# Pairs of seven block products moved between pairs of eight, and their banks read during the last pair

## The chip, the cores and the metric

One core of a Trainium2 chip runs the whole program in one launch. The metric is the device time of one execution in microseconds (us); the time before is the median of three runs. Five engines work at their own pace: TensorE (matmuls and transposes; PE in the profile), VectorE (DVE), ScalarE (ACT), GpSimd (POOL) and SyncE (SP), which issues the loads. Each runs its instructions in the order in which the program has them, and waits where an operand or a buffer isn't ready.

## What is computed

Two layers, each a mixer (a gated recurrence, differential attention and latent attention, joined and projected) and a feed-forward block, on 256 rows of 2048 numbers. The change is in the feed-forward block alone:

```python
D_MODEL = 2048
SEQ = 256
DEPTH = 2
D_FF = -(-8 * D_MODEL // (3 * 256)) * 256      # 5632
...
for l in range(DEPTH):
    ...
    x = x + mix @ w_out[l]
    h = rmsnorm(x, g_ffn[l])
    x = x + (jax.nn.silu(h @ w_gate[l]) * (h @ w_up[l])) @ w_down[l]
return rmsnorm(x, g_final)
```

All of it is float32.

## The kernel before

**Products.** The 5632 hidden columns go in eleven blocks f0 to f10 of 512. For each block a *gate-up product* multiplies the 256 rows (two row tiles t = 0, 1 of 128) with 512 columns of `w_gate` and 512 of `w_up`, over 16 blocks of 128 inputs. Its result is turned around in `hidden()` by TensorE's transposes and stored as the left side of the *down products*. The hidden blocks are taken in groups 0 to 3, 4 to 7 and 8 to 10; after each group two down products (one for each half of the 2048 output columns, again as two halves of 512) add into `x`. Both kinds are written by `paired()`.

**Precision.** A number is split in a high part and a low rest (`whi`, `wlo`): ScalarE casts (L231), VectorE subtracts (L232), and `mm3()` makes three matmuls (L237 to L239). A matmul here has 128 rows of weights and 512 columns.

**Pairs.** A product takes its input blocks two at a time. A *pair of eight* makes the eight block products (two weights, two row tiles, two input blocks) with 24 matmuls, and needs two loads of 512 KB, each split by `load_split()`. A *pair of seven* makes seven block products with 21 matmuls: it takes weighted sums of the blocks of both sides. The sums of the left side are made once (`build_sums()`); those of the weights are made for each pair by VectorE (L345 to L348, half operations of 512 columns) and split (L349, L350, L352, L354), with ScalarE's casts between (L343, L344, L351, L353). A product with sevens has five pairs of eight and three of seven: 5 x 24 + 3 x 21 = 183 matmuls. f0 of each layer has eight pairs of eight (192 matmuls). The two down products after f10 have six pairs: the first all of eight (144), the second in layer 0 with two of seven (138); in layer 1 the last is another function. In all 86 pairs of seven, in 28 products of three and one of two. The loads and weight sums of such a product, 22 tiles, pass in turn through the six buffers of `wraw`; the parts of splits go through three buffers of `whl`; of the sums there are two sets for V and W (`A_SET`) and one for gate and up (`A_GU`).

**Banks.** TensorE adds up in banks of PSUM. `acc` has five: C11, C22, C21, C12 (one for each weight half and row tile) and P1; `aux` has three, P5, P7, P6, and serves the transposes as well. A product with sevens runs all its pairs of eight first and then its three sevens. C22 is complete after the eights, the others after the last seven; `ev()` reads them: for a gate-up product two copies and ten VectorE operations, which end in silu(gate) x up in `sil`, for a down product twelve additions.

**What sets the order.** TensorE's order is the program's own. The other engines' order is made by a scheduler when the kernel is built, which gives `tc.high_priority()` work precedence. Side work is done a step at a time: each `yield` of a product calls `tick()`, which runs one step of up to two generators of `side` (in the feed-forward block `hidden()`, whose second and third step transpose two blocks each, and `xT_steps()`, which prepares the next stage's left side).

Of the kernel before, what the change touches and what calls it, by code (L numbers as in the profile page):

```python
# [21 lines left out]
P = 128  # L22
D = 2048
T = 256
NT = 2
# [12 lines left out]
SEVEN_X, SEVEN_H = (5, 6, 7), (3, 4, 5)  # L38
ARENA1, ARENA2 = 14504, 2816
# [18 lines left out]
def body(ctx: ExitStack, tc: tile.TileContext, x_in, pos_in, pvec_in, lamv_in, cst_in, w_in, w_r, w_i, w_q_b,  # L58
# [109 lines left out]

    side = []
# [25 lines left out]
    def run(gen, ticks=None):  # L195
        for i, _ in enumerate(gen):
            if ticks is None or i < ticks:
                tick()
# [102 lines left out]
    def paired(wg, wu, order, seven, part, sums, ev):  # L301
# [7 lines left out]
        C11, C22, C21, C12 = (acc() for _ in range(4))  # L309
        bank = {(0, 0): C11, (1, 1): C22, (0, 1): C21, (1, 0): C12}  # L310
        plain = ((0, 0), (0, 1), (1, 0), (1, 1)) if not seven else ((0, 0), (1, 1), (0, 1), (1, 0))
# [5 lines left out]
        for i, p in enumerate(order):  # L317
            last = i == len(order) - 1
            hl = [load_split(w[2 * p * P:(2 * p + 2) * P], 2, (512,)) for w in (wg, wu)]
            for s, t in plain:  # L320
                hi, lo = hl[s]
                for j in range(2):
                    mm3(bank[s, t], part(2 * p + j, t), (hi[:, j], lo[:, j]), i == 0 and j == 0,
                        last and j == 1 and (not seven or (s, t) == (1, 1)))
                if last and not seven:
                    read((s, t), bank[s, t])
            if last and seven:
                read("C22", C22)
            yield
        if not seven:  # L330
            return
        P1 = acc()
        P5, P7, P6 = (aux() for _ in range(3))
        for i, p in enumerate(seven):
            e, o = 2 * p, 2 * p + 1
            G, U = (load(w[2 * p * P:(2 * p + 2) * P], 2, (512,)).rearrange("p (a b) -> p a b", a=2)
# [18 lines left out]
            first, end = i == 0, i == len(seven) - 1  # L355
            S1, S2, S3, S4 = sums(p)
            mm3(P1, part(e, 0), (gh[:, 0], gl[:, 0]), first, end)
            if end:
                read("P1", P1)
            mm3(C11, part(o, 0), (gh[:, 1], gl[:, 1]), False, end)  # L360
            if end:
                read("C11", C11)
            mm3(C12, S4, (uh, ul), False, end)
            mm3(P5, S1, (vh[:, 0], vl[:, 0]), first, end)
            mm3(P7, S3, (vh[:, 1], vl[:, 1]), first, end)
            mm3(P6, S2, (wh[:, 0], wl[:, 0]), first, end)
            if end:
                read("P6", P6, P7)
# [790 lines left out]
```

## Time and profile before

| | us |
|---|---|
| median of 3 runs | 2136.89 (2136.43 to 2139.54) |
| the profiled execution | 2142.38 |
| its span, first to last instruction | 2140.6 |
| layer 0, f1 to the last down product | 694.24 |
| layer 1, f1 to the last paired down product | 656.41 |

The profile lists each engine's busy time, who waited for whom, and the instructions in order of time. A matmul's end is modelled, and matmuls overlap; so two that start 0.23 us apart are both drawn 0.39 us long. A window row gives each engine's busy time in a stretch, with the number of its instructions in brackets. The products of layer 0 begin at 335.98 (f0), 381.42 (f1), 424.56 (f2), 469.50 (f3) and 514.38 us (first down product).

### The profile page before, as it was taken

How to read it: one execution, taken by the hardware profiler on the slowest of the kernel's cores; microseconds unless marked ns; L12 is line 12 of the kernel's file. 1: busy time of each engine (PE TensorE's matmuls, PEld its weight loads, DVE VectorE, ACT ScalarE, POOL GpSimd, SP SyncE). 2: the span in 40 equal slices, each digit the busy share in tenths (PEclk: the TensorE clock that was granted, in tenths of full speed). 3: DMA queues.
4: the chain of work that ended last, by engine and by line, in shares of the span. 5: the costliest groups of instructions: out<-in, count | busy, mean ns of one | idle time of the engine just before them, and what ended most of it. 6: DMA issues, size and time to landing. Idle time of an engine off the chain costs nothing.

```text
span 2140.6 us, 27189 instructions
## 1 busy us (share of the span) xinstructions
PE 2080.3 (97%) x10044; PEld 1727.0 (81%) x10044; DVE 1681.4 (79%) x2381; ACT 1174.0 (55%) x1622; POOL 14.9 (1%) x32
## 2 busy tenths in 40 slices
PE   8999999999999999999999999999999999999998
PEld 7898888877777777777798998887777777777786
DVE  5775756789898898988775756567889888999885
ACT  5764655556455564555647545455554555555554
POOL 0000000000000000000000000000000000000000
PEclk9999999999999999999999999999999999999999
DMA  7664456555556555565565645565555655556563
GB/s 243 172 181 134 159 175 187 190 186 174 187 187 210 190 170 189 185 206 188 171 192 159 193 126 169 180 181 194 169 183 187 206 195 174 184 185 217 190 213 132
DMA packets 204213, 391.17 MB, mean 183 GB/s; under 512 B 18960, under 2 KB 36384, under 8 KB 203952
## 3 DMA queue, kind: packets, MB, share of 16 engines
q1 hardware_dynamic: 204032, 389.36, 56.7%
q8 instruction: 78, 1.28, 0.2%
q14 instruction: 55, 0.45, 0.1%
q0 software_dynamic: 48, 0.09, 0.0%
HBM read 387.30 MB, written 2.10 MB: 182 GB/s over the span
## 4 chain that ended last, share of the span: by engine, by line
PE 52%; DVE 29%; DMA 11%; issue 5%; ACT 2%; DVEq 0%; SPq 0%; ACTq 0%; POOLq 0%; POOL 0%
PE acc L238 16%; PE acc L239 16%; PE acc L237 15%; DVE wlo L232 8%; DMA wraw<-in_w_up 6%; DMA wraw<-in_w_down 4%; DVE arena L352 2%; DVE arena L354 2%; DVE wraw L346 2%; ACT whi L231 2%; DVE wraw L347 2%; DVE wraw L345 2%; DVE arena L350 2%; DVE arena L349 2%; DVE wraw L348 1%
## 5 line engine op out<-in xcount | busy, mean ns | idle before, releaser
L232 DVE TENSOR_TENSOR wlo<-wraw,whi 128x1024 fp32r<-128x1024 f32 (+2 forms) x568 | 665.4, 1179 | 310.3 <-ACT whi L231 304.6
L231 ACT CAST whi<-wraw 128x1024 fp32r<-128x1024 f32 (+2 forms) x568 | 576.2, 1015 | 547.2 <-PE acc L239 389.6
L238 PE MATMUL acc<-wlo,xTh 128*128 128x512 f32 x1248 | 487.0, 390 | 24.0 <-DVE wlo L232 23.7
L237 PE MATMUL acc<-whi,xTh 128*128 128x512 f32 x1248 | 490.4, 393 | 0.0
L239 PE MATMUL acc<-whi,xTl 128*128 128x512 f32 x1248 | 482.8, 387 | 0.0
L238 PE MATMUL acc<-wlo,hTh 128*128 128x512 f32 (+1 forms) x784 | 307.6, 392 | 14.9 <-DVE wlo L232 14.9
L237 PE MATMUL acc<-whi,hTh 128*128 128x512 f32 (+1 forms) x784 | 309.3, 395 | 0.1
L239 PE MATMUL acc<-whi,hTl 128*128 128x512 f32 (+1 forms) x784 | 305.6, 390 | 0.0
L238 PEld LDWEIGHTS acc<-wlo,xTh 128*128 128x128 f32 x1248 | 234.8, 188 | 86.9 <-DVE wlo L232 42.9
L237 PEld LDWEIGHTS acc<-whi,xTh 128*128 128x128 f32 x1248 | 234.7, 188 | 45.3
L239 PEld LDWEIGHTS acc<-whi,xTl 128*128 128x128 f32 x1248 | 234.6, 188 | 45.4
L238 PEld LDWEIGHTS acc<-wlo,hTh 128*128 128x128 f32 x784 | 148.2, 189 | 50.9 <-DVE wlo L232 23.1
L237 PEld LDWEIGHTS acc<-whi,hTh 128*128 128x128 f32 x784 | 148.2, 189 | 30.7 <-issue 1.3
L239 PEld LDWEIGHTS acc<-whi,hTl 128*128 128x128 f32 x784 | 148.2, 189 | 29.4
L351 ACT CAST arena<-wraw 128x1024 fp32r<-128x1024 f32 x86 | 90.3, 1050 | 121.6 <-DVE wraw L346 121.5
L237 PE MATMUL acc<-xTh,whi 128*128 128x256 f32 x384 | 111.4, 290 | 1.9 <-ACT xTh L484 1.0
L349 DVE TENSOR_TENSOR arena<-wraw,arena 128x1024 fp32r<-128x1024 f32 x86 | 104.9, 1220 | 9.1 <-ACT arena L343 8.3
L343 ACT CAST arena<-wraw 128x1024 fp32r<-128x1024 f32 x86 | 90.3, 1050 | 37.7 <-PE acc L239 26.9
L238 PE MATMUL acc<-xTl,whi 128*128 128x256 f32 x384 | 109.0, 284 | 1.9 <-DVE xTl L485 1.9
L239 PE MATMUL acc<-xTh,wlo 128*128 128x256 f32 x384 | 108.8, 283 | 0.5 <-DVE wlo L232 0.5
L354 DVE TENSOR_TENSOR arena<-wraw,arena 128x1024 fp32r<-128x1024 f32 x86 | 105.2, 1223 | 0.0
L352 DVE TENSOR_TENSOR arena<-wraw,arena 128x1024 fp32r<-128x1024 f32 x86 | 104.8, 1219 | 0.0
(260 smaller groups left out, 2957.1 us busy)
## 6 DMA issues: line engine op xcount, KB each, us to landing
wraw<-in_w_gate SPq DMA_DIRECT2D x176, 512.0 KB, 4.3
wraw<-in_w_up SPq DMA_DIRECT2D x176, 512.0 KB, 4.6
wraw<-in_w_down SPq DMA_DIRECT2D x176, 512.0 KB, 4.6
wraw<-in_w_out SPq DMA_DIRECT2D x64, 512.0 KB, 3.8
wraw<-in_w_in SPq DMA_DIRECT2D x48, 512.0 KB, 4.2
wraw<-in_w_in SPq DMA_DIRECT2D x48, 384.0 KB, 3.2
wraw<-in_w_in SPq DMA_DIRECT2D x32, 416.0 KB, 3.5
arena<-in_w_in SPq DMA_DIRECT2D x16, 384.0 KB, 7.4
```

The lines of the kernel that those rows point to most:

```text
L231: nc.scalar.copy(hi[:, :n], raw[:, :n])
L232: nc.vector.tensor_tensor(lo[:, :n], raw[:, :n], hi[:, :n].bitcast(F32), ALU.subtract)
L237: nc.tensor.matmul(ps, a[0], b[0], start=start, stop=False)
L238: nc.tensor.matmul(ps, a[0], b[1], start=False, stop=False)
L239: nc.tensor.matmul(ps, a[1], b[0], start=False, stop=stop)
L343: nc.scalar.copy(fl(gh), fl(G))
L345: tt(V[:, 0], U[:, 0], G[:, 0], ALU.subtract)
L346: tt(V[:, 1], U[:, 1], U[:, 0], ALU.subtract)
L349: tt(fl(gl), fl(G), f_(fl(gh)), ALU.subtract)
L351: nc.scalar.copy(fl(vh), fl(V))
L352: tt(fl(vl), fl(V), f_(fl(vh)), ALU.subtract)
L354: tt(fl(wl), fl(W), f_(fl(wh)), ALU.subtract)
```

## The change

`SEQ` writes out the order of a product's pairs: with three sevens it is eight, eight, seven, eight, seven, eight, seven, eight (`OOSOSOSO`), and it ends with an eight. The four banks of a product are taken in the order in which they are used, (0, 0), (0, 1), (1, 0), (1, 1) (weight half, row tile), and every pair of eight fills them in that order; before, products with sevens went (0, 0), (1, 1), (0, 1), (1, 0). Within a seven the products of P6, P7 and P5 stand in that order. After the last seven P1, P6, P7 and P5 are joined (stage `"P"`), while TensorE does the last eight; each of the four banks is read when its part of that eight is done. The copy of C22 by ScalarE in gate-up products is gone; the numbers of VectorE operations are as before. Ticks: none after a seven and after an eight between sevens, one more in the middle of each product's second eight; so the two steps of `hidden()` with transposes come in the middle and at the end of the second eight.

```diff
 SEVEN_X, SEVEN_H = (5, 6, 7), (3, 4, 5)
+
+SEQ = {(8, 0): "OOOOOOOO", (6, 0): "OOOOOO", (6, 2): "OOSOSO", (8, 3): "OOSOSOSO", (8, 2): "OOSOOSOO"}
...
     def run(gen, ticks=None):
-        for i, _ in enumerate(gen):
-            if ticks is None or i < ticks:
+        for i, v in enumerate(gen):
+            if v is not False and (ticks is None or i < ticks):
                 tick()
...
-        C11, C22, C21, C12 = (acc() for _ in range(4))
-        bank = {(0, 0): C11, (1, 1): C22, (0, 1): C21, (1, 0): C12}
-        plain = ((0, 0), (0, 1), (1, 0), (1, 1)) if not seven else ((0, 0), (1, 1), (0, 1), (1, 0))
+        bank, ps = {}, []
 
         def read(stage, *banks):
             with tc.high_priority(offset=AHEAD):
                 ev(stage, *banks)
 
-        for i, p in enumerate(order):
-            last = i == len(order) - 1
+        def eight(i, p, last):
             hl = [load_split(w[2 * p * P:(2 * p + 2) * P], 2, (512,)) for w in (wg, wu)]
-            for s, t in plain:
-                hi, lo = hl[s]
-                for j in range(2):
-                    mm3(bank[s, t], part(2 * p + j, t), (hi[:, j], lo[:, j]), i == 0 and j == 0,
-                        last and j == 1 and (not seven or (s, t) == (1, 1)))
-                if last and not seven:
-                    read((s, t), bank[s, t])
-            if last and seven:
-                read("C22", C22)
-            yield
-        if not seven:
-            return
-        P1 = acc()
-        P5, P7, P6 = (aux() for _ in range(3))
-        for i, p in enumerate(seven):
+            for s in range(2):
+                for t in range(NT):
+                    if i == 0:
+                        bank[s, t] = acc()
+                    hi, lo = hl[s]
+                    for j in range(2):
+                        mm3(bank[s, t], part(2 * p + j, t), (hi[:, j], lo[:, j]), i == 0 and j == 0, last and j == 1)
+                    if last:
+                        read((s, t), bank[s, t])
+                if i == 1 and s == 0:
+                    yield
+
+        def seven_of(i, p, end):
             e, o = 2 * p, 2 * p + 1
+            if i == 0:
+                ps.extend([acc()] + [aux() for _ in range(3)])
+            P1, P6, P7, P5 = ps
...
             S1, S2, S3, S4 = sums(p)
-            mm3(P1, part(e, 0), (gh[:, 0], gl[:, 0]), first, end)
+            mm3(P1, part(e, 0), (gh[:, 0], gl[:, 0]), i == 0, end)
             if end:
                 read("P1", P1)
-            mm3(C11, part(o, 0), (gh[:, 1], gl[:, 1]), False, end)
+            mm3(bank[0, 0], part(o, 0), (gh[:, 1], gl[:, 1]), False, False)
+            mm3(bank[1, 0], S4, (uh, ul), False, False)
+            mm3(P6, S2, (wh[:, 0], wl[:, 0]), i == 0, end)
+            mm3(P7, S3, (vh[:, 1], vl[:, 1]), i == 0, end)
+            mm3(P5, S1, (vh[:, 0], vl[:, 0]), i == 0, end)
+            mm3(bank[0, 1], part(o, 1), (wh[:, 1], wl[:, 1]), False, False)
             if end:
-                read("C11", C11)
-            mm3(C12, S4, (uh, ul), False, end)
-            mm3(P5, S1, (vh[:, 0], vl[:, 0]), first, end)
-            mm3(P7, S3, (vh[:, 1], vl[:, 1]), first, end)
-            mm3(P6, S2, (wh[:, 0], wl[:, 0]), first, end)
-            if end:
-                read("P6", P6, P7)
-            mm3(C21, part(o, 1), (wh[:, 1], wl[:, 1]), False, end)
-            if end:
-                read("end", C21, C12, P5)
-            yield
+                read("P", P6, P7, P5)
+
+        todo = [*order]
+        done = 0
+        n = len(order) + len(seven)
+        for i in range(n):
+            if SEQ[n, len(seven)][i] == "S":
+                seven_of(done, seven[done], done == len(seven) - 1)
+                done += 1
+                yield False
+            else:
+                p = todo.pop(0)
+                for _ in eight(len(order) - len(todo) - 1, p, i == n - 1):
+                    yield
+                yield not 0 < done < len(seven)
...
+        q12, q22 = (at(A_U + i * 512, 512) for i in range(2))
 
         def ev(stage, a, b=None, c=None):
...
+            if stage == "P1":
+                nc.scalar.copy(sil[0], a)
+            elif stage == "P":
+                tt(q12, sil[0], a, ALU.add)
+                tt(sil[1], q12, b, ALU.add)
+                tt(q22, sil[1], c, ALU.add)
+                tt(q12, q12, c, ALU.add)
             else:
-                tt(sil[1], u3, a, ALU.add)
-                gate(1, sil[1])
-                tt(u2, u2, c, ALU.add)
-                tt(u2, u2, b, ALU.add)
-                tt(u3, u3, c, ALU.add)
-                tt(u3, u3, o22, ALU.add)
-                up(0, u2)
-                up(1, u3)
+                s, t = stage
+                if seven:
+                    v = (sil[t], q12 if t == 0 else q22)[s]
+                    tt(v, v, a, ALU.add)
+                    a = v
+                if s == 0:
+                    nc.scalar.activation(sil[t], a, AF.Silu, scale=rs[:, t:t + 1])
+                else:
+                    nc.vector.scalar_tensor_tensor(sil[t], a, rs[:, t:t + 1], sil[t], ALU.mult, ALU.mult)
...
+        p1, u2, u3 = (at(v, 512) for v in (A_SIL, A_U, A_U + 512))
+
+        def add_x(t, g, a):
+            v = x[:, t, c + g * 512:c + g * 512 + 512]
+            tt(v, v, a, ALU.add)
...
         def ev(stage, a, b=None, e=None):
-            if isinstance(stage, tuple):
+            if stage == "P1":
+                nc.scalar.copy(p1, a)
+            elif stage == "P":
+                tt(u2, p1, a, ALU.add)
+                tt(u3, u2, b, ALU.add)
+                add_x(0, 0, p1)
+                add_x(1, 0, u3)
+                tt(u2, u2, e, ALU.add)
+                tt(u3, u3, e, ALU.add)
+                add_x(0, 1, u2)
+                add_x(1, 1, u3)
+            else:
                 g, t = stage
                 add_x(t, g, a)
                 done(t, g)
...
```

The first place is VectorE at the end of product f2 (`arena2` holds partial results, `acc` and `aux` are banks, L232 splits the weights of f3's pairs of eight, L395 to L406 and L383 read). Before:

```order
L232 TENSOR_TENSOR wlo_4335<-wraw_4332,whi_4334 128x1024
L232 TENSOR_TENSOR wlo_4341<-wraw_4338,whi_4340 128x1024
L398 TENSOR_TENSOR arena2_95<-arena2_95,aux_4195 128x512
L232 TENSOR_TENSOR wlo_4371<-wraw_4368,whi_4370 128x1024
L399 TENSOR_TENSOR arena2_95<-arena2_95,aux_4194 128x512
L401 TENSOR_TENSOR arena2_95<-arena2_95,acc_3988 128x512
L403 TENSOR_TENSOR arena2_95<-arena2_95,aux_4193 128x512
L405 TENSOR_TENSOR arena2_95<-arena2_95,aux_4193 128x512
L404 TENSOR_TENSOR arena2_95<-arena2_95,acc_3989 128x512
L406 TENSOR_TENSOR arena2_95<-arena2_95 128x512
L383 SCALAR_TENSOR_TENSOR arena2_95<-arena2_95,rs_3287 128x512 x2
L232 TENSOR_TENSOR wlo_4377<-wraw_4374,whi_4376 128x1024
```

After (there L235 splits, L393 to L405 read, L346, L347 and L350 are the sums and a split of f3's first seven):

```order
L393 TENSOR_TENSOR arena2_95<-arena2_95,aux_4084 128x512
L394 TENSOR_TENSOR arena2_95<-arena2_95,aux_4085 128x512
L395 TENSOR_TENSOR arena2_95<-arena2_95,aux_4085 128x512
L400 TENSOR_TENSOR arena2_95<-arena2_95,acc_3997 128x512
L346 TENSOR_TENSOR wraw_4438<-wraw_4436,wraw_4434 128x512
L347 TENSOR_TENSOR wraw_4438<-wraw_4436 128x512
L400 TENSOR_TENSOR arena2_95<-arena2_95,acc_4004 128x512
L350 TENSOR_TENSOR arena_3292<-wraw_4434,arena_3292 128x1024
L400 TENSOR_TENSOR arena2_95<-arena2_95,acc_4011 128x512
L400 TENSOR_TENSOR arena2_95<-arena2_95,acc_4018 128x512
L405 SCALAR_TENSOR_TENSOR arena2_95<-arena2_95,rs_3287 128x512 x2
L235 TENSOR_TENSOR wlo_4335<-wraw_4332,whi_4334 128x1024
```

The reads were in one stretch with three splits among them. Now the join of the `aux` banks comes first, the reads of the four banks alternate with work for f3's first seven, and the splits of f3's first pairs of eight, but for the gate half of the first, stand behind the last read. In most other gate-up products the split of the first pair's up half stands ahead of the read of the last bank.

The second place is VectorE inside f2, from its second seven on. Before:

```order
L345 TENSOR_TENSOR wraw_4239<-wraw_4237,wraw_4235 128x512
L346 TENSOR_TENSOR wraw_4239<-wraw_4237 128x512
L347 TENSOR_TENSOR wraw_4240<-wraw_4237,wraw_4239 128x512
L348 TENSOR_TENSOR wraw_4240<-wraw_4235,wraw_4240 128x512
L352 TENSOR_TENSOR arena_3292<-wraw_4239,arena_3292 128x1024
L354 TENSOR_TENSOR arena_3292<-wraw_4240,arena_3292 128x1024
L349 TENSOR_TENSOR arena_3292<-wraw_4235,arena_3292 128x1024
L350 TENSOR_TENSOR arena_3292<-wraw_4237,arena_3292 128x512
L345 TENSOR_TENSOR wraw_4278<-wraw_4276,wraw_4274 128x512
L346 TENSOR_TENSOR wraw_4278<-wraw_4276 128x512
```

After (L346 to L355 are a seven, L235 are splits for an eight):

```order
L235 TENSOR_TENSOR wlo_4203<-wraw_4200,whi_4202 128x1024
L235 TENSOR_TENSOR wlo_4209<-wraw_4206,whi_4208 128x1024
L346 TENSOR_TENSOR wraw_4240<-wraw_4238,wraw_4236 128x512
L347 TENSOR_TENSOR wraw_4240<-wraw_4238 128x512
L348 TENSOR_TENSOR wraw_4241<-wraw_4238,wraw_4240 128x512
L350 TENSOR_TENSOR arena_3292<-wraw_4236,arena_3292 128x1024
L349 TENSOR_TENSOR wraw_4241<-wraw_4236,wraw_4241 128x512
L351 TENSOR_TENSOR arena_3292<-wraw_4238,arena_3292 128x512
L353 TENSOR_TENSOR arena_3292<-wraw_4240,arena_3292 128x1024
L355 TENSOR_TENSOR arena_3292<-wraw_4241,arena_3292 128x1024
L235 TENSOR_TENSOR wlo_4283<-wraw_4280,whi_4282 128x1024
L235 TENSOR_TENSOR wlo_4289<-wraw_4286,whi_4288 128x1024
```

Sevens followed each other; now two splits for a pair of eight stand between them, and two more follow the third.

The third place is ScalarE in f3, at the second set of transposed hidden blocks (`aux_4454` before, `aux_4416` after) and the casts around it. Before:

```order
L343 CAST arena_3292<-wraw_4545 128x1024
L509 COPY arena2_95<-aux_4404 128x512
L344 CAST arena_3292<-wraw_4547 128x512
L231 CAST whi_4476<-wraw_4474 128x1024
L481 CAST arena_3292<-arena2_95 128x512
L231 CAST whi_4506<-wraw_4504 128x1024
L481 CAST hTh_4326<-aux_4454 128x512
L351 CAST arena_3292<-wraw_4549 128x1024
L509 COPY arena2_95<-aux_4454 128x512
```

After (L469 and L497 read the bank, L344 casts the second seven's gate block):

```order
L469 CAST hTh_4324<-aux_4390 128x512
L234 CAST whi_4481<-wraw_4479 128x1024
L497 COPY arena2_95<-aux_4390 128x512
L469 CAST hTh_4324<-aux_4416 128x512
L344 CAST arena_3292<-wraw_4509 128x1024
L469 CAST arena_3292<-arena2_95 128x512
L497 COPY arena2_95<-aux_4416 128x512
L345 CAST arena_3292<-wraw_4511 128x512
L352 CAST arena_3292<-wraw_4513 128x1024
```

The two reads of the bank stood about the cast of a seven whose products were still to come; now the cast of the second seven's gate block stands between them, and the first seven's products use the same three `aux` banks.

## Rows read from the trace of the kernel before

**Rows 1.** The page, part 1: busy us, share of the span, instructions
```profile
PE 2080.3 (97%) x10044; PEld 1727.0 (81%) x10044; DVE 1681.4 (79%) x2381; ACT 1174.0 (55%) x1622; POOL 14.9 (1%) x32
```

**Rows 2.** TensorE in order of time: start us, length us, instruction [idle before, releaser]
```profile
381.42 0.39 PE L237 MATMUL acc<-whi,xTh 128*128 128x512 f32 x1
...
392.08 0.39 PE L239 MATMUL acc<-whi,xTl 128*128 128x512 f32 x1
392.31 0.60 PE L475 MATMUL aux<-ident,arena 128*128 128x128 f32 x4
392.66 0.48 PE L237 MATMUL acc<-whi,xTh 128*128 128x512 f32 x1
...
476.30 0.39 PE L237 MATMUL acc<-whi,xTh 128*128 128x512 f32 x1
478.04 0.50 PE L238 MATMUL acc<-wlo,xTh 128*128 128x512 f32 x1 [1.35 <-DVE wlo L232]
```

**Rows 3.** Windows: length, busy us (count) of PE, PEld, DVE, ACT, POOL; PEclk, DMA, GB/s
```profile
335.98:381.42 45.44, 45.44 (x209) 37.64 (x208) 29.21 (x45) 28.13 (x42) 0.69 (x1) 1.00 0.63 185
...
424.56:469.50 44.94, 43.59 (x192) 34.86 (x191) 39.38 (x51) 25.45 (x30) 0.00 (x0) 1.00 0.56 185
469.50:514.38 44.88, 43.17 (x193) 34.94 (x191) 41.35 (x57) 26.25 (x32) 0.00 (x0) 1.00 0.57 183
...
1004.76:1038.71 33.95, 33.91 (x154) 27.75 (x152) 26.15 (x37) 16.96 (x23) 0.00 (x0) 1.00 0.67 228
...
381.42:1075.66 694.24, 670.42 (x2949) 540.52 (x2948) 603.88 (x747) 373.73 (x440) 0.00 (x0) 1.00 0.57 188
1442.49:2098.90 656.41, 636.43 (x2795) 513.15 (x2794) 573.82 (x708) 352.56 (x408) 0.00 (x0) 1.00 0.58 191
```

**Rows 4.** TensorE's waits, layer 0's stretch, then layer 1's: us, times, longest
```profile
PE acc L238 <- DVE wlo L232: 20.3, 25, 1.5
PE aux L237 <- DVE xTl L485: 1.7, 1, 1.7
PE acc L238 <- DVE arena L349: 1.4, 5, 0.4
...
PE acc L238 <- DVE wlo L232: 18.3, 24, 1.5
PE acc L238 <- DVE arena L349: 1.6, 5, 0.3
```

**Rows 5.** VectorE in order of time at the end of product f2
```profile
463.05 1.22 DVE L349 TENSOR_TENSOR arena<-wraw,arena 128x1024 fp32r<-128x1024 f32 x1
464.19 0.69 DVE L350 TENSOR_TENSOR arena<-wraw,arena 128x512 fp32r<-128x512 f32 x1
464.79 1.22 DVE L352 TENSOR_TENSOR arena<-wraw,arena 128x1024 fp32r<-128x1024 f32 x1
...
467.06 0.68 DVE L395 TENSOR_TENSOR arena<-arena,acc 128x512 f32<-128x512 f32 x1
...
475.44 1.41 DVE L383 SCALAR_TENSOR_TENSOR arena<-arena,rs 128x512 f32<-128x512 f32 x2
476.77 2.35 DVE L232 TENSOR_TENSOR wlo<-wraw,whi 128x1024 fp32r<-128x1024 f32 x2
482.00 1.23 DVE L232 TENSOR_TENSOR wlo<-wraw,whi 128x1024 fp32r<-128x1024 f32 x1 [2.87 <-ACT whi L231]
```

**Rows 6.** VectorE, the small sums of one hidden block
```profile
447.73 0.28 DVE L515 TENSOR_TENSOR arena<-arena 128x128 f32<-128x128 f32 x1
447.93 0.29 DVE L517 TENSOR_TENSOR arena<-arena 128x128 f32<-128x128 f32 x1
```

**Rows 7.** A window, and the loads of 424 to 520 us (KB, us to landing)
```profile
424.00:426.00 2.00, 2.00 (x11) 1.65 (x10) 2.00 (x3) 0.12 (x1) 0.00 (x0) 1.00 1.04 379
...
wraw<-in_w_up SPq DMA_DIRECT2D x13, 512.0 KB, 4.8
```

More of the change, by code (lines that the diff above doesn't have):

```diff
@@ L354, in paired @@
                 tt(fl(wl), fl(W), f_(fl(wh)), ALU.subtract)
-            first, end = i == 0, i == len(seven) - 1
             S1, S2, S3, S4 = sums(p)
-            mm3(P1, part(e, 0), (gh[:, 0], gl[:, 0]), first, end)
+            mm3(P1, part(e, 0), (gh[:, 0], gl[:, 0]), i == 0, end)
             if end:
                 read("P1", P1)
-            mm3(C11, part(o, 0), (gh[:, 1], gl[:, 1]), False, end)
-            if end:
-                read("C11", C11)
-            mm3(C12, S4, (uh, ul), False, end)
@@ L374, in gate_up @@
     def gate_up(wg, wu, rs, sil, seven):
         tt = nc.vector.tensor_tensor
-        u2, u3, o22 = (at(A_U + i * 512, 512) for i in range(3))
-        def gate(t, v):
-            nc.scalar.activation(sil[t], v, AF.Silu, scale=rs[:, t:t + 1])
-        def up(t, v):
-            nc.vector.scalar_tensor_tensor(sil[t], v, rs[:, t:t + 1], sil[t], ALU.mult, ALU.mult)
-        def ev(stage, a, b=None, c=None):
-            if stage in ((0, 0), (0, 1)):
-                gate(stage[1], a)
-            elif stage in ((1, 0), (1, 1)):
-                up(stage[1], a)
-            elif stage == "C22":
-                nc.scalar.copy(o22, a)
-            elif stage == "P1":
-                nc.scalar.copy(sil[1], a)
-            elif stage == "C11":
-                tt(sil[0], sil[1], a, ALU.add)
-                gate(0, sil[0])
-            elif stage == "P6":
-                tt(u2, sil[1], a, ALU.add)
-                tt(u3, u2, b, ALU.add)
-            else:
-                tt(sil[1], u3, a, ALU.add)
-                gate(1, sil[1])
-                tt(u2, u2, c, ALU.add)
-                tt(u2, u2, b, ALU.add)
-                tt(u3, u3, c, ALU.add)
-                tt(u3, u3, o22, ALU.add)
-                up(0, u2)
-                up(1, u3)
@@ L433, in ev @@
                 done(t, g)
-            elif stage == "C22":
-                add_x(1, 1, a)
-            elif stage == "P1":
-                nc.scalar.copy(p1, a)
-            elif stage == "C11":
-                add_x(0, 0, p1, a)
-                done(0, 0)
-            elif stage == "P6":
-                tt(u2, p1, a, ALU.add)
-                tt(u3, u2, b, ALU.add)
-            else:
-                add_x(1, 0, a, u3)
-                done(1, 0)
-                tt(u2, u2, e, ALU.add)
-                add_x(0, 1, b, u2)
-                done(0, 1)
-                tt(u3, u3, e, ALU.add)
-                add_x(1, 1, u3)
-                done(1, 1)
         def part(k, t):
```

5 lines of the change are left out of this document (removed).

## The prediction

> **What bounds the kernel now.** I read the page's busy times first. TensorE is busy 2080.3 us of 2140.6, 97%, and VectorE 1681.4 us, 79% [rows 1]. That reads as a kernel with nothing left on TensorE, so I asked next how fast matmuls follow each other when nothing is missing. From 381.42 to 392.08 us, two pairs of eight, there are 47 intervals: 10.66 / 47 = 0.2268 us from start to start, while each is drawn 0.39 us long [rows 2]. A busy TensorE can therefore hide a lost tenth of a microsecond, and the measure to use is starts, not busy time. Four transposes in a group take 0.35 us (392.31 to 392.66) [rows 2].
>
> With that the stages are weighed by the window rows [rows 3]. Product f2 of layer 0 has 183 matmuls and two groups of transposes: 183 x 0.2268 + 2 x 0.35 = 42.2 us; it took 44.94. f3 took 44.88. The products without pairs of seven lose far less: f0 (192 matmuls, four groups) should take 44.9 and took 45.44, the down product at 1004.76 (144 matmuls, two groups) 33.4 and took 33.95. So about 0.5 us is lost in a product whatever it is, and 2.7 us where pairs of seven stand. Summed: from f1 to the end of layer 0's last product the row counts 2949 TensorE instructions, by the code 2844 matmuls of 512 columns and 26 groups of four transposes, 645.0 + 9.1 = 654.1 us, against 694.24: 40.1 us lost. Layer 1, f1 to its last paired product: 2706 matmuls and 22 groups, 621.4 against 656.41: 35.0. Together **75.1 us** in 31 products; less 31 x 0.5 that every product loses, **60 us** can be won. Nothing outside these stretches is touched.
>
> The waits say for what: 49 waits on the split of a weight block (wlo), 38.6 us of 43.3 in the two stretches, the longest 1.5 us [rows 4]. The Trainium skill (Perfetto Trace Analysis, section Identifying the Most-Contended Engine) says that matmul busy time is a poor measure of headroom because matmuls are pipelined; by the waits alone I would put the most that can be won at 43.3 us, by starts at 60. Starts and windows agree with that page here, and I use 60.
>
> Where the waits lie is seen at the end of f2. VectorE does the splits of three pairs of seven without a break, the reads of the banks from 467.06 to 476.77, and only behind them, at 476.77, the split of the second pair's up block; TensorE stands from 476.30 to 478.04 for it (1.74 less 0.23: 1.5 us). Then VectorE has nothing to do until 482.00 [rows 2, 5]. The same engine is late and idle within 6 us: it is a matter of order, since in f2 it is busy 39.38 of 44.94 us and in f3 41.35 of 44.88 [rows 3].
>
> **What the change does, priced.** No matmul and no VectorE operation comes or goes: ten reads for a gate-up product before and after, twelve for a down product. ScalarE loses one copy of 0.58 us in each of 20 gate-up products; it is busy 26 of 45 us [rows 3], so that is worth nothing.
>
> *Pairs of seven between pairs of eight.* A whole split costs VectorE 1.14 us (463.05 to 464.19), a half operation 0.60 (464.19 to 464.79), the two closing multiplications 1.33 together (475.44 to 476.77) [rows 5]. A pair of seven: 3 x 1.14 + 5 x 0.60 = 6.42 us, for 21 matmuls or 4.76 us of TensorE. A pair of eight: 2.28 us for 5.44 of TensorE. In a row, three sevens are 19.3 us against 14.3; alternating, a seven and an eight are 8.7 against 10.2. Whole product f3, with the hidden blocks of f2 (two splits of 0.60, two sets of sums of four 0.20 plus 0.60 [rows 6]): 10 x 1.14 + 3 x 6.42 + 8 x 0.60 + 1.33 + 1.2 + 2.8 = 40.8 us, against TensorE's 42.2. It fits with 1.4 us to spare; f2, with one set of sums, with 2.8.
>
> *Does each step arrive in time?* Clock from the start of the last pair of eight, TensorE running without a stop. The last block product but one of the last seven (P5) is out at about -0.5; four reads follow to 1.9. In most boundaries then stand two first differences and one split of the next product's first seven, the three reads of banks that are done by 4.1, and the up split of the next product's first eight, done at 7.2. TensorE wants it at 5.44 + 13 x 0.2268 = 8.4: 1.2 us to spare. The last split of the next product's first seven is done at 15.5 and wanted at 19.0, that of the second at 26.8 (28.2 in f3) and wanted at 29.2, of the third at 35.5 (36.9) and wanted at 39.4. Nothing is late there. The changed order of the banks helps too: the up block is now wanted half way through a pair, 1.36 us later than the quarter at which it is wanted before.
>
> *Loads.* Blocks of seven now have one set of buffers: the next one's load starts when this one's differences are made, at 13.1, and is wanted at 18.8. 5.7 us, against 4.8 from issue to landing [rows 7]. At a boundary six loads are let go from -9.4 to -4.6, 3.1 MB; the DMA moves 379 GB/s when it has work in hand [rows 7], so they are in by about +1, when they are wanted. I price this at nothing, and take it up as a rival.
>
> *What stays or is new.* (a) In f2 to f3 and f6 to f7 the order puts the up split behind the read of the last bank and both multiplications: that bank is out at 5.6, 5.6 + 0.6 + 1.33 + 1.14 = 8.7 at the earliest and 9.1 with the reads before it, against 8.4. 0.3 to 0.7 us in four boundaries; 0.5 each, 2 us. (b) The three auxiliary banks are now handed from the transposes to the first seven soon after. In f3 and f7 ScalarE's copy of the second transposed bank stands behind the cast of the second seven's gate block, which waits for the first seven's second block product: 1.5 + 0.95 + 0.5 + 0.59 = 3.5 to 3.8 us into the seven, where TensorE wants the bank at 3.4. 0.5 each, four times, 2 us. (c) Layer 0's last product does transposes for the next layer at the same banks; it waits 1.7 us there now [rows 4], and 3 us of its loss I leave. (d) No row shows how much VectorE loses in chains of dependent operations once it is filled to 97%. Bounds: nothing (the spare time takes it) and 1.4 us, f3's whole spare, in each of the 29 products with sevens, 41 us. I take 0.5 us in the 10 products with sums, where the spare is smallest: 5 us.
>
> **Sum.** 60 - 2 - 2 - 3 - 5 = 48 us. The profiled execution took 2142.38 us, 5.5 above the median of 2136.89; the gain is taken off both, 2094 for an execution like it and 2136.9 - 48 = **2089** for the median.
>
> **Rivals.** *VectorE becomes the bound.* For it: 41.35 us busy in f3 [rows 3], and most of its waits are in chains with ScalarE that the interleaving doesn't shorten. Against it: its largest idle stretches (2.87 us at 482.00 [rows 5]) come from having run out of buffers, which the new order ends. If three quarters of its idle time stayed, f2 would take 39.38 + 4.2 = 43.6, f3 41.35 + 2.6 = 44.0: 1.1 us won in each of 29 products, 32 us: 2105.
>
> *Slower: reads and new work block the splits behind them.* VectorE runs its instructions in the order in which they stand, as the row at 476.77 shows, which waited behind eight reads. At most gate-up boundaries a difference or split of the next seven now stands ahead of the bank reads and the up split, and it waits for a load. The Trainium skill (TensorE: Matmul & The Clock Gate, section on the 16 x 32x32 array) has ScalarE and VectorE as strictly first in, first out; the rows agree, and by that rule one late load holds up all. Its price: if the six loads went at the mean rate, 188 GB/s over layer 0's stretch [rows 3], the last would land at 7.3 instead of 1, and TensorE would stand 5 us at each of 18 boundaries: 90 - 48, 42 us slower, 2179. It decides from a landing at about 4.9 (the 2.2 that are spared and 48 / 18), that is below some 220 GB/s. Against it: the 379 GB/s.
>
> *The stalls only move.* The same operations, and VectorE nearly full: each late split at the end becomes one in the middle. 2137.
>
> **How the numbers follow.** The forecast, 2075 to 2100: 0.66. VectorE bound, 2100 to 2125: 0.22. Only moved: 0.05. Slower: 0.07. Low end: all 60 us and a little, 2075. High end: into the first rival until a tenth is left above, 2113. About 0.2%, 4 us, is what a measurement can tell from no change: faster 0.88, same 0.05, slower 0.07.
>
> **What would show it.** Windows of f2 and its like at 42.5 to 43.3 us; waits on wlo down from 38.6 us to under 10; VectorE busy above 93% in f3; no 2.9 us idle stretch at the start of a product; a wait of TensorE on an aux bank in f3. I am wrong if the windows stay above 44 us, if VectorE waits on loads ahead of bank reads, or if waits appear at the start of each pair of seven.

## The result, and the profile after

The changed kernel takes 2077.97 us, median of four runs (2076.18 to 2078.26), against 2137.84 for the kernel before beside it (2136.43 to 2139.54): a ratio of 0.9718, 95% interval 0.9701 to 0.9735. 60 us are won where 48 were forecast; the time lies 11 us under the forecast and inside its range. The profiled execution took 2076.18, span 2074.2. Its part 1 of the page, against [rows 1], and the shares by engine of the chain that ended last:

```profile
PE 2054.9 (99%) x10044; PEld 1732.3 (84%) x10044; DVE 1678.9 (81%) x2381; ACT 1163.4 (56%) x1602; POOL 14.9 (1%) x32
...
PE 90%; DVE 5%; DMA 2%; issue 1%; ACT 1%; SPq 0%; DVEq 0%; POOLq 0%; POOL 0%; ACTq 0%
```

TensorE does the same 10044 instructions. Its busy share rose by two points while the span fell by 66 us: a share of 97% was no sign that nothing was left. In the kernel before the chain was 52% PE, 29% DVE and 11% DMA; it is now almost TensorE alone.

The windows, with the columns of [rows 3]: f0, f2, f3, the second down product (no transposes in it), f5 and the first down product after f10 of layer 0, and the two stretches from f1 to the last paired product:

```profile
333.39:378.83 45.44, 45.44 (x210) 37.60 (x208) 30.90 (x47) 28.81 (x43) 0.69 (x1) 1.00 0.60 175
421.47:463.92 42.45, 42.45 (x192) 35.13 (x191) 39.73 (x51) 24.46 (x30) 0.00 (x0) 1.00 0.60 198
463.92:507.39 43.47, 43.02 (x192) 34.98 (x191) 40.12 (x55) 24.17 (x31) 0.00 (x0) 1.00 0.59 194
...
549.83:591.31 41.48, 41.48 (x184) 34.35 (x183) 37.27 (x46) 21.69 (x23) 0.00 (x0) 1.00 0.62 203
632.79:676.71 43.92, 42.87 (x193) 34.98 (x192) 40.81 (x50) 25.12 (x29) 0.00 (x0) 1.00 0.59 192
...
973.03:1006.65 33.62, 33.62 (x154) 27.81 (x153) 22.88 (x32) 18.04 (x23) 0.00 (x0) 1.00 0.54 172
378.83:1040.82 661.99, 658.70 (x2945) 542.90 (x2944) 602.35 (x748) 366.43 (x429) 0.73 (x3) 1.00 0.60 197
1406.38:2032.41 626.03, 625.13 (x2795) 516.19 (x2794) 571.25 (x706) 346.66 (x398) 0.00 (x0) 1.00 0.61 201
```

f2 went from 44.94 to 42.45 us, f3 from 44.88 to 43.47. The stretches went from 694.24 to 661.99 and from 656.41 to 626.03, together 62.6 us. By the prediction's count of matmuls and transposes they needed 654.1 + 621.4 us. One of layer 0's 26 groups of transposes now begins where the stretch ends, so they need 0.35 us less, and of the 75.1 us lost before 12.9 are left: 62.2 us are won there. (The two profiled executions differ by 66 us in their spans and the medians by 60; the one before took 4.5 us more than the median given here, the one after 1.8 less, and some 4 us of the 66 lie in stages that the change doesn't touch.)

TensorE's waits in the two stretches, as in [rows 4]:

```profile
PE acc L241 <- DVE wlo L235: 1.9, 3, 1.1
PE aux L240 <- DVE xTl L473: 1.2, 1, 1.2
...
PE acc L241 <- DVE wlo L235: 0.7, 2, 0.3
```

The waits on splits went from 49 (38.6 us) to 5 (2.6 us). VectorE still waits in these stretches, but for shorter times: of idle times of 2 us or more it had 34 before and has 3.

### The profile page after: what moved, and what is told of

The parts are those of the page before. It is cut to its first block, busy times and chain, and to the rows that moved or that the text cites. A ratio compares the mean times of both kernels' runs of the same rounds, so it can differ in the third digit from the quotient of the medians.

```text
span 2074.2 us, 27308 instructions
## 1 busy us (share of the span) xinstructions
PE 2054.9 (99%) x10044; PEld 1732.3 (84%) x10044; DVE 1678.9 (81%) x2381; ACT 1163.4 (56%) x1602; POOL 14.9 (1%) x32
## 4 chain that ended last, share of the span: by engine, by line
PE 90%; DVE 5%; DMA 2%; issue 1%; ACT 1%; SPq 0%; DVEq 0%; POOLq 0%; POOL 0%; ACTq 0%
PE acc L241 26%; PE acc L240 26%; PE acc L242 26%; PE aux L240 3%; PE aux L241 2%; PE aux L242 2%; PE aux L463 2%; DVE wlo L235 1%; DMA wraw<-in_w_down 1%; DVE arena L350 1%; DVE x L423 1%; PE aux L946 1%; DVE arena L400 0%; PE aux L891 0%; PE aux L890 0%
## 5 line engine op out<-in xcount | busy, mean ns | idle before, releaser
L235 DVE TENSOR_TENSOR wlo<-wraw,whi 128x1024 fp32r<-128x1024 f32 (+2 forms) x568 | 662.1, 1177 | 257.8 <-ACT whi L234 256.1
L241 PE MATMUL acc<-wlo,xTh 128*128 128x512 f32 x1248 | 481.5, 386 | 2.6 <-DVE wlo L235 2.6
L241 PE MATMUL acc<-wlo,hTh 128*128 128x512 f32 (+1 forms) x784 | 303.4, 387 | 0.0
L344 ACT CAST arena<-wraw 128x1024 fp32r<-128x1024 f32 x86 | 90.5, 1053 | 190.0 <-PE acc L242 82.7
L354 ACT CAST arena<-wraw 128x1024 fp32r<-128x1024 f32 x86 | 90.6, 1054 | 117.2 <-DVE wraw L349 117.2
L350 DVE TENSOR_TENSOR arena<-wraw,arena 128x1024 fp32r<-128x1024 f32 x86 | 104.8, 1218 | 8.1 <-ACT arena L344 7.9
L352 ACT CAST arena<-wraw 128x1024 fp32r<-128x1024 f32 x86 | 90.3, 1051 | 36.4 <-DVE wraw L347 36.0
L355 DVE TENSOR_TENSOR arena<-wraw,arena 128x1024 fp32r<-128x1024 f32 x86 | 104.8, 1218 | 0.0
```

What stands on the lines that cost most here:

```text
L235: nc.vector.tensor_tensor(lo[:, :n], raw[:, :n], hi[:, :n].bitcast(F32), ALU.subtract)
L241: nc.tensor.matmul(ps, a[0], b[1], start=False, stop=False)
L344: nc.scalar.copy(fl(gh), fl(G))
L350: tt(fl(gl), fl(G), f_(fl(gh)), ALU.subtract)
L352: nc.scalar.copy(fl(vh), fl(V))
L354: nc.scalar.copy(fl(wh), fl(W))
```

## The experiments

The change has three parts: the **bank order** (the up block of a pair of eight is wanted after 12 matmuls, not after 6: 1.36 us later), the **interleaving** of sevens and eights, and the **reads** of the banks behind a last eight instead of behind the last seven. The first group of kernels takes them apart; a second tests the terms of the sum. All but the second kernel are made from the changed one, so they keep its other edits, which no run takes apart: the order within a seven, the joining of the `aux` banks and the new places of the transposes. The kernel before ran at a median of 2132.8 to 2139.7 us beside these runs, so gains are compared by the ratios. A **stall** is a time from one start of TensorE to the next that is longer than the usual 0.227 us; what is over counts as its length, and it is put down to the matmul that it follows.

**Bank order and reads, no interleaving.**

```diff
-(6, 2): "OOSOSO", (8, 3): "OOSOSOSO"
+(6, 2): "OOOSSO", (8, 3): "OOOOSSSO"
```

> The changed kernel with its three sevens in a row again, ahead of the last pair of eight (OOOOSSSO and OOOSSO); the banks are still read during that last eight, and the order of the banks is the new one. Three theories of where the 60 us came from. I, interleaving: what counts is that sevens alternate with eights, 8.7 us of VectorE against 10.2 of TensorE instead of 19.3 against 14.3; then most of the gain goes, 2115 to 2135 us. R, the reads: what counts is that the banks are read behind an eight and not behind the last seven; then the gain stays but for some 0.4 us a product in which the third seven waits for the one set of gate and up buffers, 2080 to 2095. B, the order of the banks: what counts is that the up block of a pair is wanted half way instead of at a quarter; the same, 2080 to 2095.

Measured: 2090.72 us against 2132.8, ratio 0.9804 (0.9789 to 0.9818), so most of the gain stays, as R and B had it. 15.2 us are left in stalls of over 0.25 us, 11.7 of them within the three sevens in a row, at their 22nd, 43rd and 52nd matmul: this is what interleaving takes away once the rest is there.

**Bank order alone**, in the kernel before:

```diff
-        plain = ((0, 0), (0, 1), (1, 0), (1, 1)) if not seven else ((0, 0), (1, 1), (0, 1), (1, 0))
+        plain = ((0, 0), (0, 1), (1, 0), (1, 1))
```

> The kernel before with one line changed: every pair of eight fills its banks in the order (0,0), (0,1), (1,0), (1,1), so the up block is wanted 6 matmuls, 1.36 us, later. Sevens still follow in a row and the banks are read after the last of them. Theory B (order of the banks): the waits of TensorE before, up to 1.5 us each and nearly all at the seventh matmul of a pair, shrink by 1.36 us each; 2085 to 2100. Theories I (interleaving) and R (reads behind an eight): the late splits are late all the same, 2125 to 2140; R adds that bank (0,1) is now wanted before the old one has been read, which could make it slower than before, up to 2150.

Measured: 2096.78, ratio 0.9834 (0.982 to 0.9849): one line, and 36 of the 60 us. This was the surprise of the study. TensorE's largest waits with it, over the whole program:

```profile
PE acc L238 <- DVE arena L349: 7.7, 17, 1.5
PE acc L238 <- DVE wlo L232: 5.5, 8, 1.1
```

Waits on splits of pairs of eight (wlo, L232) fell from 38.6 us to 5.5; those on the pairs of seven (L349) rose from 2.9 to 7.7. By starts, the kernel before had 63 stalls of over 0.25 us, 53.8 us in all, and 41 of them, 42.7 us, were at the 7th matmul of one of a product's four first pairs of eight, which is where the up block was wanted. VectorE was late there by at most 1.5 us and idle a little later ([rows 5]), so 1.36 us more of time took nearly all of it.

**Bank order and interleaving, all banks read behind the last seven.**

```diff
-(6, 2): "OOSOSO", (8, 3): "OOSOSOSO"
+(6, 2): "OOSOOS", (8, 3): "OOSOOSOS"
...
+            if end:
+                for s in range(2):
+                    for t in range(NT):
+                        read((s, t), bank[s, t])
```

> The changed kernel with sevens between eights but a seven at the end (OOSOOSOS and OOSOOS), the four banks read after that seven; order of the banks new. Theory R (reads behind an eight): bank (0,1) of the next product is wanted 1.4 us after the end and read at about 2.1, and the second pair's up split stands behind all reads, at about 8.4, when it is wanted; 0.7 to 1.5 us in each of 29 products, 2098 to 2125. Theories I (interleaving) and B (order of the banks): within 2078 to 2090.

Measured: 2092.78, ratio 0.9813 (0.9798 to 0.9827). The time falls between the two ranges; the place speaks for R, since it is the old banks that are in the way. 14.6 us are left in such stalls, 11.3 of them at the 6th, 12th and 18th matmul of a product, for banks of the last product that are not yet read; of waits on splits of pairs of eight one is left, 0.5 us.

**Interleaving and reads, without the bank order**:

```diff
-            for s in range(2):
-                for t in range(NT):
+            for q in range(4):
+                s, t = (q % 2, q // 2) if seven and not last else (q // 2, q % 2)
```

> The changed kernel, but every pair of eight of a product with sevens, except its last, takes the banks (0, 0), (1, 0), (0, 1), (1, 1): the up block is wanted after 6 matmuls, as before the change, not after 12, 1.36 us earlier. Order of pairs and reads as changed. This is the change without the part that gave 36 of 60 us alone. Theory A (the prediction's clock): the middle eights have slack enough; at the start of a product the spare 1.2 us become -0.16 and the 0.5 us of f3 and f7 become 1.9: about 0.2 x 25 + 1.4 x 4 = 10 us more than the changed kernel, 2083 to 2093, the whole of it at the 7th matmul of a product's first eight. Theory B (the bank order's part is its own and adds up): about 36 us more, 2105 to 2120, with waits on up splits in the middle eights too.

Measured: 2079.57 against 2136.38, ratio 0.9734 (0.9719 to 0.9749). That is 57 of the 60 us without the part that gives 36 alone, faster than either theory had it. The expected place shows it in f1 alone (0.62 and 0.73 us at the 7th matmul), not in f3 and f7, where the scheduler's order now has the split of the up half ahead of the last bank's read; three stalls of 0.39 to 0.79 us stand in second eights.

**Interleaving alone** (the last two kernels' edits together, the order `OOSOOSOS` and the up block wanted after 6 matmuls):

> Only the interleaving: pairs of seven stand between pairs of eight, but a product ends with its last seven and all banks are read behind it, and the up block of a pair of eight is wanted after 6 matmuls, as before the change. If the three parts were each worth something of their own and added up (36 for the bank order alone, 18 for interleaving and 20 for the reads on top of others), about 18 us are won: 2115 to 2122 on a before of 2137. If they are substitutes (each gives VectorE's splits time at the same places, so that the first of them takes most): the up split of the next product stands behind the reads and is wanted 1.36 us too early in 28 products, some 1.5 us each: 2078 + 42, 2110 to 2125, but stalls only there, at the 7th matmul of a product's first eight. The two differ in the next run.

Measured: 2130.16 against 2139.7 (seven runs, 2128.89 to 2140.98), ratio 0.9964 (0.9947 to 0.9982): 8 us, by the interval 4 to 11. Both theories had asked for more, 12 to 27. Its waits of TensorE:

```profile
PE acc L241 <- DVE wlo L235: 13.8, 16, 1.5
PE acc L240 <- DVE x L428: 6.0, 8, 0.8
PE acc L240 <- DVE arena L405: 5.3, 15, 1.5
```

The second and third row are banks which the last product's reads (L428, L405) have not yet freed; by starts such stalls, at the 6th, 12th and 18th matmul of a product, come to 20.0 us, and those on splits to 18.1, nearly all of them at the 7th matmul of the fourth pair of eight. So a product that ends on a seven pays at its successor's start; why the split of the fourth pair is late was not tested. (The order in which this kernel takes the banks, and that of the last and the next kernel, isn't that of the kernel before, and part of the 20 us may be due to that: 8 us is what it gave, not a clean price.)

**Reads behind an eight alone** (`OOOOSSSO`, up block wanted after 6 matmuls):

> Only the reads behind an eight: four or three pairs of eight, the pairs of seven in a row, one last pair of eight; the up block of a pair of eight, but the last, is wanted after 6 matmuls, as before the change. If the parts add up: 20 us won, 2115 to 2120. If they are substitutes: the reads and the next up split are no longer in a row with three sevens' splits, which was the place of the longest waits (1.5 us at nearly every boundary), and most of the gain comes from this alone, 40 us or more: 2085 to 2100. If the row of three sevens is what costs (19.3 us of VectorE against 14.3 of TensorE): it stays, and under 10 us are won, 2127 or more.

Measured: 2119.4, ratio 0.9908 (0.9891 to 0.9924): 20 us, as the first of the three theories had it. 38 us of stalls are left, 35.9 of them at the 7th matmul of the first, third and fourth pair of eight of a product. One of them is in f2's fourth eight. VectorE, then TensorE, in order of time:

```profile
442.25 1.22 DVE L353 TENSOR_TENSOR arena<-wraw,arena 128x1024 fp32r<-128x1024 f32 x1
443.39 0.69 DVE L470 TENSOR_TENSOR arena<-arena,arena 128x512 fp32r<-128x512 f32 x1
443.99 1.22 DVE L235 TENSOR_TENSOR wlo<-wraw,whi 128x1024 fp32r<-128x1024 f32 x1
...
443.99 0.39 PE L240 MATMUL acc<-whi,xTh 128*128 128x512 f32 x1
445.27 0.50 PE L241 MATMUL acc<-wlo,xTh 128*128 128x512 f32 x1 [0.89 <-DVE wlo L235]
```

A split for the first seven (L353), which TensorE wants some 7 us later (30 matmuls), stands ahead of the up split that it wants at 444.2. Wanted 1.36 us later, as in the first experiment, it would have been in time.

The eight combinations of the three parts, as gains in us (1 less the ratio, times 2137.84):

| | without bank order | with bank order |
|---|---|---|
| neither | 0 | 35.5 |
| interleaving | 7.7 | 40.0 |
| reads behind an eight | 19.7 | 41.9 |
| both | 56.9 | 60.3 |

The parts are neither a sum nor plain substitutes. Interleaving and reads need each other: 7.7 and 19.7 apart, 56.9 together. The bank order is worth 35.5 alone, 32 on top of the interleaving, 22 on top of the reads, and 3.4 when both are there, where the intervals overlap.

**How much of VectorE is spare.** Eight, then three additions of 512 columns more in the second seven of each product:

```diff
+                if i == 1:
+                    for _ in range(8):
+                        tt(at(A_U + 1024, 512), V[:, 0], V[:, 1], ALU.add)
```

> The changed kernel with eight needless VectorE additions of 512 columns (0.60 us each, 4.8 us) in the second seven of each of the 29 products with sevens; it measures how much spare time VectorE has. By the tally behind the prediction (40.8 us of VectorE in f3 against 42.2 of TensorE): 1.4 us to spare in f3 and f7, 2.8 in products with one set of sums, 4.2 with none, 4.7 in products without hidden work; so it loses 3.4 x 4 + 2.0 x 6 + 0.6 x 10 + 0.1 x 8, about 33 us, 2100 to 2120. If VectorE loses time in chains once it is full (term d of the prediction), the spare is smaller by up to 1.4 us everywhere: 2125 to 2160. If the spare is larger than counted: under 2095.

> The changed kernel with three additions of 512 columns more (0.60 us each, into an unused buffer) in the second pair of seven of each of 29 products: 1.8 us more of VectorE a product, where eight gave 2.0 us for 4.8. Theory A (VectorE's spare time is a pool that is used up first, 2.8 us a product by that run): little is lost outside f3 and f7, where the spare is smallest: 0 to 8 us, 2077 to 2086. Theory B (what counts is where the work stands, a fixed share of it is lost at any amount): 2.0 / 4.8 x 1.8 x 29 = 22 us, 2095 to 2105.

Measured: eight, 2137.26, ratio 1.0022 (1.0013 to 1.0032); three, 2078.46, ratio 0.9728 (0.9712 to 0.9744). Three of them, 1.8 us a product, cost nothing that can be told; eight, 4.8 us a product, cost 59 us by the medians and 65 by the ratios, 2.0 to 2.2 a product. So the spare time is used up first, and it is 2.6 to 2.8 us a product on average. I had reckoned 3.7 and missed by 17 us at least: 2137.26 lies in the range that I had given for time lost in chains once VectorE is full. Whether it is chains was not tested. The waits with eight, then the window of f2:

```profile
PE aux L241 <- DVE arena L355: 19.5, 20, 1.2
PE acc L241 <- DVE wlo L235: 12.6, 8, 2.1
PE acc L241 <- DVE arena L350: 7.6, 10, 1.0
...
421.52:466.61 45.09, 43.38 (x192) 34.89 (x191) 45.09 (x61) 25.28 (x31) 0.00 (x0) 1.00 0.56 187
```

Over half of them lie on the sevens behind the added work (L355, L350), and VectorE is busy for all of f2's 45.09 us: it is now behind, not in the wrong order. Less eight times 0.60, that is 40.3 us of VectorE for an f2 that took 42.45.

**The loads.** Five buffers of `wraw` in place of six.

```diff
-    wraw_p = pool("wraw", 6)
+    wraw_p = pool("wraw", 5)
```

> The changed kernel with five buffers of 512 KB for loads and weight sums in place of six. A load of a block of seven had 5.7 us from the freeing of its buffer to its use by the prediction's clock, against 4.8 from issue to landing. Forecast by that clock: a load starts one tile's turn later, some 2 to 3 us, and is 1 to 2 us late in each of 86 pairs of seven: 80 to 170 us more in the two stretches of the feed-forward blocks. By the rival (a late load holds up all that stands behind it on VectorE) the waits of TensorE name splits of blocks whose own load had landed, VectorE waits for loads, and the loss is above that, over 200 us. If loads have more room than I reckoned: under 30 us. The other stages use these buffers too; the two stretches are compared by their windows alone.

One run: 2111.17, span 2108.6. The stretches took 680.91 and 641.27 us, 34 us more than the changed kernel: less than half of my lower figure, and a little over the 30 that I had put for loads with more room. The first two rows are ScalarE's longest waits for loads; then follows f2's first seven on ScalarE and on TensorE:

```profile
ACT whi L234 <- DMA wraw<-in_w_up: 88.0, 59, 3.2
...
ACT whi L234 <- DMA wraw<-in_w_down: 44.7, 33, 2.7
...
435.39 1.05 ACT L234 CAST whi<-wraw 128x1024 fp32r<-128x1024 f32 x1 [0.56 <-DMA wraw<-in_w_up]
436.35 0.57 ACT L469 CAST hTh<-aux 128x512 fp32r<-128x512 f32 x1
437.08 1.05 ACT L344 CAST arena<-wraw 128x1024 fp32r<-128x1024 f32 x1 [0.15 <-DMA wraw<-in_w_gate]
438.34 0.59 ACT L497 COPY arena<-aux 128x512 f32<-128x512 f32 x1 [0.21 <-DVE hTl L470]
...
438.98 0.50 PE L240 MATMUL aux<-arena,xSh 128*128 128x512 f32 x1 [1.21 <-ACT arena L497]
```

With six buffers the two casts of `whi` wait 9.6 and 5.7 us for loads in the whole program. With five, a load is late by a little nearly everywhere, and TensorE waits 1.21 us not for that load but for a bank that ScalarE reads behind it. Of 32.5 us of stalls in the stretches 24.3 stand at this place, the 63rd matmul of a product; there the profile names ScalarE's copy of the bank for 10.4 us of waits and VectorE's read of it for 8.6. That is the mechanism of the slower rival, at the `aux` banks, with a price: 34 us for one buffer of six.

**What is left in f3 and f7.**

```diff
-        with tc.high_priority(offset=AHEAD):
+        with tc.high_priority(offset=AHEAD + 60):
             nc.scalar.copy(hi[:, :n], raw[:, :n])
...
-        a = at(A_U, 4, P)
+        turn[0] ^= 1
+        a = at(A_U + 1024 * turn[0], 4, P)
```

> The changed kernel with two edits against the 0.5 and 0.26 us that are left in f3 and f7: the split of a loaded block goes ahead of bank reads and sums that are ready at the same time, and the two sets of sums of a product use two scratch buffers in turn, so that ScalarE's copy of the second transposed bank needn't wait for the first set. Theory A (these stalls come from the order of VectorE's and ScalarE's work): the stalls at the 13th and 63rd matmul of f3 and f7 go, 4 x 0.76 = 3 us, 2073 to 2077. Rival (VectorE is too full there, 40 of 43.5 us, and the stalls move to the reads of the banks or to a later split): no change, 2076 to 2080.

Measured: 2075.96, ratio 0.9717 (0.9702 to 0.9731), the same as the changed kernel's. The stalls of 0.5 us at the 13th matmul are gone in all four products, and new ones of 0.4 to 0.57 us stand at the 103rd, where TensorE waits for a split of the second seven; the 0.26 us at the 63rd stayed. The two theories' times overlap and can't be told apart; by the places the rival was right for the first edit: the stall only moved, to a later split. The second edit, for ScalarE's copy, did nothing, and the cause of that wait stays open. No kernel of this study is measurably better than the changed one.

## Why the prediction came out as it did

**The measure.** Counting starts, not waits, was right. By the waits 43.3 us could have been won; 62.2 went in the two stretches. The Trainium skill (Perfetto Trace Analysis, section Identifying the Most-Contended Engine) has matmul busy time as a poor measure of headroom; the trace agrees: the same 10044 instructions are drawn 2080.3 us before and 2054.9 after.

**The term that was mis-sized** is the deduction of 31 x 0.5 = 15.5 us that "a product loses whatever it is". The second down product shows 41.48 us for its 183 matmuls, 183 x 0.2267: nothing lost. f2, with two groups of transposes, loses 0.25 (42.45 against 42.2). I had taken the floor from f0, whose 0.49 is the same loss for four groups (45.44 before and after), and from the down product at 1004.76, which itself still held stalls: it went from 33.95 to 33.62. With some 0.25 us in the 23 products with transposes and nothing in the other eight, under 6 us are lost in this way, not 15.5. So 10 us too much was deducted here, and 5 more by (d) below; (b) and (c) were put too high by 2 together, and loads and the starts behind a stall, about 2 us that I had not put down, go the other way. Together that is 14 to 15 us in the two stretches, as the windows have it. The medians won only 12 us more than the 48 forecast, since the two profiled executions lie further apart than they do.

**The smaller terms.** (a) The up split in f2 to f3 and f6 to f7 was put at 0.3 to 0.7 us late, four times, 2 us. It is 0.50 in three of them and 0.65 in one. VectorE at the end of f2, to be laid beside [rows 5], and TensorE:

```profile
461.85 0.68 DVE L400 TENSOR_TENSOR arena<-arena,acc 128x512 f32<-128x512 f32 x1
462.45 1.22 DVE L350 TENSOR_TENSOR arena<-wraw,arena 128x1024 fp32r<-128x1024 f32 x1
463.58 1.28 DVE L400 TENSOR_TENSOR arena<-arena,acc 128x512 f32<-128x512 f32 x2
464.78 1.41 DVE L405 SCALAR_TENSOR_TENSOR arena<-arena,rs 128x512 f32<-128x512 f32 x2
466.10 3.49 DVE L235 TENSOR_TENSOR wlo<-wraw,whi 128x1024 fp32r<-128x1024 f32 x3
...
466.64 0.39 PE L240 MATMUL acc<-whi,xTh 128*128 128x512 f32 x1
467.37 0.50 PE L241 MATMUL acc<-wlo,xTh 128*128 128x512 f32 x1 [0.34 <-DVE wlo L235]
```

The last eight begins at 458.48; the split wanted 8.4 us later, at 466.87, ends at 467.3: 467.37 - 466.64 less 0.23 is 0.50 us. In other products the split stands ahead of the last reads, and nothing is lost.

(b) ScalarE's copy of the second transposed bank was put at 0.5 us in f3 and f7. ScalarE, then TensorE at its third auxiliary product:

```profile
477.95 1.06 ACT L344 CAST arena<-wraw 128x1024 fp32r<-128x1024 f32 x1 [0.70 <-PE acc L242]
478.90 0.62 ACT L469 CAST arena<-arena 128x512 fp32r<-128x512 f32 x1
479.42 0.58 ACT L497 COPY arena<-aux 128x512 f32<-128x512 f32 x1
...
480.05 0.50 PE L240 MATMUL aux<-arena,xSh 128*128 128x512 f32 x1
```

The place is right and the cast of the second seven's gate block is what stands ahead, but the loss is 0.26 us, four times 1.0. (c) Layer 0's last product loses 1.8 us, 1.36 of it in one wait at the `aux` banks; 3 were left for it. (d) The 5 us for chains in a full VectorE came to nothing: whatever is lost in them, the spare time took it, as it took the three extra additions.

**Loads**, priced at nothing, cost 1.2 us once: f5 of layer 0. Its first seven's gate block was the fifth of six loads issued in a row, from 620.10 to 625.25 us, and landed 6.3 us after its issue. ScalarE, VectorE and TensorE:

```profile
630.46 1.05 ACT L344 CAST arena<-wraw 128x1024 fp32r<-128x1024 f32 x1 [4.79 <-DMA wraw<-in_w_gate]
...
631.54 1.23 DVE L350 TENSOR_TENSOR arena<-wraw,arena 128x1024 fp32r<-128x1024 f32 x1 [2.32 <-ACT arena L344]
...
635.68 1.22 DVE L235 TENSOR_TENSOR wlo<-wraw,whi 128x1024 fp32r<-128x1024 f32 x1
...
636.95 0.50 PE L241 MATMUL acc<-wlo,xTh 128*128 128x512 f32 x1 [1.05 <-DVE wlo L235]
```

The late load holds the cast, the cast holds L350, and behind L350 stand three reads and the up split. It is the chain of the slower rival, seen once; in layer 1 the same f5 took 42.45 us. VectorE does wait for loads ahead of bank reads, which I had named as a sign that I am wrong. L350 waits in this way eight times, by 0.15 to 2.32 us, and only the longest cost TensorE anything; the next, 1.52 us at 1786.84, was taken by the spare time.

**The sum as it came out**: of 75.1 us, 62.2 were won. Of the 12.9 left, (a) took 2.2, (b) 1.0, (c) 1.8, f5 1.2, and 5 to 6 the transposes; the rest is the slower starts behind the stalls in f3, f5 and f7 (0.11 us each) and rounding.

**The reason was told in the wrong proportion.** "The changed order of the banks helps too" was one sentence without a price. It is the largest single part, 36 us in one line, although nearly worthless beside the other two. The interleaving, to which the prediction gave its first and longest argument, gives 8 us alone. Its rate argument came true only together with the moved reads, and then the two give 57. The sum couldn't see this, since it priced the state after, not the parts; it came out near because the state after was right, and high because nearly all its errors were on the cautious side. The Trainium skill (Perfetto Trace Analysis, section Optimization Strategy) says that interleaving stretches with different limits may help, and that the same gap repeating can mean too few buffers. Here the interleaving alone gave 8 us, and the repeating gap of up to 1.5 us went with the same six buffers, by order alone.

**The rivals.** VectorE isn't the bound: f2 took 42.45 and not 43.6, and 1.8 us of work a product more cost nothing. It is near, though: 4.8 us more undo the whole gain. Stalls only moved in the last experiment, not in the change. Of the marks, waits on wlo, the idle stretches and the wait on an aux bank came as told, and f2's window lies at 42.45 just under the 42.5 to 43.3; VectorE's share in f3 is 40.12 of 43.47 us, 92%, just under the 93% that I had asked for, since f3 kept 1 us of stalls.

## What to carry to other kernels

A bottleneck engine that is busy 97% may still lose 3%: take the time from start to start in a quiet stretch, multiply by the count, and compare with the length of the stage. Where an engine that feeds it is late by about 1 us and idle a little later, first look whether the late operand can be wanted later within the same step, since that may be an exchange of two inner loops, which here gave 36 us where the whole new schedule gave 60. And try the parts of a change in pairs before crediting one: two parts worth 8 and 20 us alone gave 57 together.

## What was unexpected of the hardware

A stall of TensorE costs more than its wait: the first matmul after one takes 0.34 us to the next start (467.37 to 467.71, where 0.23 is usual), and so in the kernel before (478.04 to 478.38). The same is seen after a group of transposes, where the first matmul takes 0.32 (476.27 to 476.59): twice 0.09 is 0.18 of the 0.25 us that a product with two groups loses; the rest is spread over matmuls near the groups, which follow at up to 0.236 us. Otherwise the pace is even: 183 matmuls in 41.48 us, in each of the eight products of the changed kernel that have no transposes.
